# Loads of a batch of row pairs split by column halves in a tuned weight-gradient matmul

## The chip, the cores and the metric

One core of a Trainium2 chip. The metric is the device time of one execution, in microseconds (us). The kernel before takes 163.06 us, the median of two runs (162.97 and 163.16).

## The reference

```python
batch, m, k, n = 16, 512, 1024, 768      # input: [16, 512, 1024], grad_output: [16, 512, 768], float32

def reference(input, grad_output):
    return np.einsum('bmk,bmn->kn', input, grad_output).astype(np.float32)
```

With batch and m taken as one axis this is one matrix product: out[k, n] is the sum over 8192 rows of X[row, k] * G[row, n], with X of 8192 x 1024 and G of 8192 x 768. The kernel computes it in bf16 with float32 sums.

## The kernel before, in words

The 8192 rows are cut into 64 tiles of 128 rows, and these are taken two at a time: 32 pairs, numbered 0 to 31. A pair's rows lie in two tiles of on-chip memory (SBUF), `xp` (128 partitions x 2 x 1024, bf16) and `gp` (128 x 2 x 768, bf16). The DMA turns float32 into bf16 on the way.

*Loads.* POOL issues nearly all of them, in the order of the pairs (lines 108 to 126). From pair 2 on (`MERGED = 2`) a pair comes in two transfers: line 114 loads G, line 115 loads X. Partition p takes rows 2p and 2p+1 of the pair's 256, which lie side by side in memory, so that each partition reads one contiguous run (6 KB of G, 8 KB of X, float32). Pairs 0 and 1 come row tile by row tile (lines 119 and 121), and the first tile of G and the first two of X come as float32 on the queues of SP and ACT (lines 88 to 91) and are rounded by DVE and ACT (line 212). In the program as built, POOL's transfers take turns on eight semaphores: from the ninth on, each waits until the one eight before it has landed. A pair also waits for its buffer, of which there are 14 (`PAIRS_HELD`).

*Two kinds of pairs.* `LOADS` gives each pair a kind. An "s" pair (0 to 6, 30 and 31) is multiplied plainly, one row tile at a time. The output is cut into four quarters by halves of K and of N: A and B are the upper half of K, C and D the lower; A and C use the right half of G's columns (`LEFT` is `slice(NH, N)`), B and D the left. Each quarter is four matmuls of 128 x 384 per row tile (`Q = 4`), so 16 per tile and 32 per pair. A "P" pair (7 to 29) takes 7 products in place of 8, as Strassen's method does with 2 x 2 blocks, the blocks being the two row tiles and the two column halves: D, A and five more sums m, n, o, p and q, 28 matmuls in all. Its operands are sums and differences of the blocks. DVE makes them in five steps per pair, `sum_g1` (line 139) and `sum_g2` (144) from `gp`, `sum_x1` (149), `sum_x2` (153) and `sum_x3` (158) from `xp`. `sum_g1` reads all of `gp`, `sum_x1` all of `xp`; some products read the raw blocks (the function `operands`).

*Order.* `ORDER` is written out by hand: each step names a stream (A to D, m to q), the item up to which it goes on, and how its banks of PSUM are drained. A number ahead of the letter is how many sums (or later steps of putting the shares together) DVE does first. PE, DVE, ACT and POOL run the instructions in just this order (`manual_schedule`). PE accumulates a stream in four banks of PSUM (line 338). When a step closes, DVE adds the banks to float32 sums in SBUF (line 358) or ACT copies them there (354), having carried the earlier sum into the bank beforehand (297). Near the end DVE adds the shares of m to q to the quarters (195), and SP stores each finished block (line 361); the last block is multiplied and stored in two pieces (lines 393 to 403).

The lines that the steps below touch: 114 and 115 (the loads of pairs 2 to 31), 139 and 149 (the first sums on a pair's G and X), 338 (the matmuls and their weight loads).

Of the kernel before, what the change touches and what calls it, by code (L numbers as in the profile page):

```python
# [46 lines left out]
def kernel(  # L47
# [6 lines left out]
    nc = tc.nc  # L54
# [3 lines left out]
    B, M, K = input.shape  # L58
    _, _, N = grad_output.shape
    S = B * M // P  # L60
    KH = K // 2
    NH = N // 2
# [5 lines left out]
    X = input.rearrange("b m k -> (b m) k")  # L68
    G = grad_output.rearrange("b m n -> (b m) n")
# [38 lines left out]
    for u, kind in enumerate(LOADS):  # L108
        pool = pairs if u else head
        xp = pool.tile([P, 2, K], bf16, name="xp", tag="xp")  # L110
        gp = pool.tile([P, 2, N], bf16, name="gp", tag="gp")
        if u >= MERGED:
            rows = slice(2 * u * P, 2 * (u + 1) * P)
            nc.gpsimd.dma_start(out=gp, in_=G[rows, :].rearrange("(p m) n -> p m n", m=2))  # L114
            nc.gpsimd.dma_start(out=xp, in_=X[rows, :].rearrange("(p m) k -> p m k", m=2))  # L115
        for h in range(2):
            s = 2 * u + h
            if s > 0 and u < MERGED:
                nc.gpsimd.dma_start(out=gp[:, h, :], in_=G[s * P : (s + 1) * P, :])
            if s > 1 and u < MERGED:  # L120
                nc.gpsimd.dma_start(out=xp[:, h, :], in_=X[s * P : (s + 1) * P, :])
            if kind == "s":
                items.append(("s", xp[:, h, :], gp[:, h, :]))
        if kind == "P":
            items.append(("P", xp, gp))
        xg.append((xp, gp))
# [326 lines left out]
```

## Time and profile before

| what | value |
|---|---|
| median of 2 runs | 163.06 us (162.97 to 163.16) |
| the profiled execution: first to last instruction (span) | 161.1 us |
| granted TensorE clock | 1.000 |
| one load of G / of X from pair 2 on | 384 KB / 512 KB as written, median 16.7 / 16.8 us from issue to landing |
| POOL's issue of one such load | 0.53 us |
| one sum on DVE: line 139, 149 | 752 ns, 685 ns |
| matmul of 128 x 384, mean | 326 to 327 ns as shown; consecutive ones overlap |
| HBM read / written | 58.72 MB / 3.15 MB |

The profile is one execution, and the table's time of it is its span; the runs' time holds what lies around it too. PE is TensorE's matmuls, PEld its weight loads, DVE VectorE, ACT ScalarE, POOL GpSimd, SP SyncE. In the row of slices the span is cut into 40 equal parts, and a digit is the busy share in tenths (9 is 90% or more). The DMA queues' rows give packets, megabytes and the packets' time as a share of 16 engines; several packets can be under way on one engine, so that a share may exceed 100%. A waits row says who waited for whom: microseconds in total, times, longest. A timeline row is start, duration, engine, line, operation, and in brackets the idle time before it with what ended it.

### The profile page before, as it was taken

Reading aid. Unit: us, or ns where it says so; the run is one execution under the profiler, and the core shown is the slowest. Engines: PE = TensorE matmul, PEld = TensorE weight load, DVE = VectorE, ACT = ScalarE, POOL = GpSimd, SP = SyncE. Lnnn points to the kernel's source line nnn. Section 1 sums busy time; section 2 is a strip of 40 time slices with the busy share of each in tenths; the row PEclk is TensorE's granted clock in tenths of the full one; section 3 lists DMA queues with packets and bytes.
Section 4 is the critical chain, followed back from the end, with each engine's and each line's share of the span. In section 5 each row is a group of like instructions: output and inputs, shape, how many; then the busy total and the mean of one; then the engine's idle time right before and its main releaser. Section 6 shows DMA issues by size and latency. Waiting matters only on the chain.

```text
span 161.1 us, 2769 instructions
## 1 busy us (share of the span) xinstructions
PE 157.0 (97%) x944; PEld 92.7 (58%) x944; DVE 140.7 (87%) x267; ACT 117.9 (73%) x278; POOL 34.8 (22%) x69
## 2 busy tenths in 40 slices
PE   8999999999999999999999999999999999999991
PEld 3365665556555565556655665556655665555561
DVE  0645888889799999999998999999989998999982
ACT  3735357545589899978998897997795667988730
POOL 7442222122222212222212222221222100000000
PEclk9999999999999999999999999999999999999999
DMA  5999999999999999999999999999999999900695
GB/s 176 297 210 214 213 214 216 212 215 212 214 213 212 212 212 216 212 213 211 214 212 217 212 215 213 213 213 213 213 212 213 213 214 213 202 21 0 239 354 191
DMA packets 12398, 33.40 MB, mean 207 GB/s; under 512 B 1376, under 2 KB 4192, under 8 KB 12384
## 3 DMA queue, kind: packets, MB, share of 16 engines
q0 software_dynamic: 9360, 28.64, 89.8%
q1 hardware_dynamic: 2592, 3.47, 6.2%
q10 hardware_dynamic: 432, 1.11, 1.8%
q8 instruction: 7, 0.11, 0.3%
q14 instruction: 7, 0.06, 0.1%
HBM read 58.72 MB, written 3.15 MB: 384 GB/s over the span
## 4 chain that ended last, share of the span: by engine, by line
PE 97%; DVE 0%; issue 0%
PE bank L338 94%; PE bank L97 3%; PE bank L393 0%; DVE acc L401 0%
## 5 line engine op out<-in xcount | busy, mean ns | idle before, releaser
L338 PEld LDWEIGHTS <-xp 128*128 128x128 bf16 x650 | 63.3, 98 | 44.4 <-DVE xp L212 1.5
L338 PE MATMUL bank<-gp,xp 128*128 128x384 bf16 x468 | 81.0, 327 | 0.0
L354 ACT COPY macc<-bank 128x384 f32<-128x384 f32 x91 | 39.3, 491 | 9.8 <-PE bank L338 9.4
L358 DVE TENSOR_TENSOR acc<-bank,acc 128x384 f32<-128x384 f32 x80 | 39.6, 550 | 5.2 <-PE bank L338 4.8
L338 PEld LDWEIGHTS <-xe 128*128 128x128 bf16 x276 | 26.9, 98 | 17.9 <-DVE xe L149 0.2
L354 ACT COPY acc<-bank 128x384 f32<-128x384 f32 x57 | 24.7, 484 | 13.9 <-PE bank L338 13.9
L297 ACT COPY bank<-macc 128x384 f32<-128x384 f32 x73 | 33.0, 493 | 1.6 <-DVE acc L358 0.9
L338 PE MATMUL bank<-ge,xp 128*128 128x384 bf16 x182 | 33.5, 326 | 0.0
L338 PE MATMUL bank<-gp,xe 128*128 128x384 bf16 x184 | 32.4, 326 | 0.0
L297 ACT COPY bank<-acc 128x384 f32<-128x384 f32 x47 | 21.5, 491 | 8.7 <-DVE acc L358 7.0
L115 POOL DMA_DIRECT2D xp<-in_input_dram x30 | 16.0, 532 | 52.1 <-DMA xp<-in_input_dram 28.9
L114 POOL DMA_DIRECT2D gp<-in_grad_output_dram x30 | 16.0, 533 | 38.1 <-PE bank L338 17.2
L358 DVE TENSOR_TENSOR macc<-bank,macc 128x384 f32<-128x384 f32 x35 | 18.0, 550 | 0.8 <-PE bank L338 0.8
L139 DVE TENSOR_TENSOR ge<-gp 128x1152 bf16<-128x1152 bf16 x23 | 17.3, 752 | 0.6 <-DMA gp<-in_grad_output_dram 0.5
L149 DVE TENSOR_TENSOR xe<-xp 128x1024 bf16<-128x1024 bf16 x23 | 15.8, 685 | 2.1 <-DMA xp<-in_input_dram 2.1
L195 DVE TENSOR_TENSOR acc<-acc,macc 128x768 f32<-128x768 f32 (+1 forms) x20 | 16.1, 871 | 0.0
L338 PE MATMUL bank<-ge,xe 128*128 128x384 bf16 x92 | 15.9, 326 | 0.0
L158 DVE TENSOR_TENSOR xp<-xp 128x1024 bf16<-128x1024 bf16 x23 | 15.7, 684 | 0.0
L144 DVE TENSOR_TENSOR gp<-gp 128x768 bf16<-128x768 bf16 x23 | 12.7, 554 | 0.5
L153 DVE TENSOR_TENSOR xe<-xp 128x512 bf16<-128x512 bf16 x23 | 9.6, 418 | 0.0
L356 DVE COPY acc<-bank 128x384 f32<-128x384 f32 x6 | 3.2, 555 | 3.2 <-PE bank L338 3.1
L212 DVE CAST gp<-gf 128x192 bf16<-128x192 f32 (+1 forms) x2 | 0.7, 330 | 4.3 <-DMA gf<-in_grad_output_dram 4.3
(20 smaller groups left out, 19.9 us busy)
## 6 DMA issues: line engine op xcount, KB each, us to landing
xp<-in_input_dram POOLq DMA_DIRECT2D x30, 512.0 KB, 16.8
gp<-in_grad_output_dram POOLq DMA_DIRECT2D x30, 384.0 KB, 16.7
out_dram<-acc SPq DMA_DIRECT2D x15, 192.0 KB, 2.4
xf<-in_input_dram ACTq DMA_DIRECT2D x2, 512.0 KB, 4.8
gp<-in_grad_output_dram POOLq DMA_DIRECT2D x3, 192.0 KB, 6.4
xp<-in_input_dram POOLq DMA_DIRECT2D x2, 256.0 KB, 7.7
gf<-in_grad_output_dram SPq DMA_DIRECT2D x2, 192.0 KB, 4.2
out_dram<-acc SPq DMA_DIRECT2D x1, 128.0 KB, 1.9
```

Source lines behind the costliest of these rows:

```text
L114: nc.gpsimd.dma_start(out=gp, in_=G[rows, :].rearrange("(p m) n -> p m n", m=2))
L115: nc.gpsimd.dma_start(out=xp, in_=X[rows, :].rearrange("(p m) k -> p m k", m=2))
L139: nc.vector.tensor_add(out=ge.rearrange("p a n -> p (a n)"), in0=g[:, 0 : 3 * NH], in1=g[:, NH : 4 * NH])
L144: nc.vector.tensor_sub(out=g[:, 0::3, :], in0=g[:, 0::3, :], in1=g[:, 2:0:-1, :])
L149: nc.vector.tensor_add(out=xe[:, 0:2, :].rearrange("p a k -> p (a k)"), in0=xp[:, 0, :], in1=xp[:, 1, :])
L153: nc.vector.tensor_add(out=extra[i][0][:, 2, :], in0=xp[:, 0, 0:KH], in1=xp[:, 1, KH:K])
L158: nc.vector.tensor_sub(out=x[:, 1:3, :], in0=x[:, 1:3, :], in1=x[:, 0::3, :])
L195: op(out=dst, in0=dst, in1=src)
L297: nc.scalar.copy(out=bank, in_=sum_of(p, q))
L338: nc.tensor.matmul(bank, stat, mov, start=opening and j == 0 and not carried, stop=close and j == len(items_now) - 1, skip_group_check=car ...
L354: nc.scalar.copy(out=dst, in_=bank)
L358: nc.vector.tensor_add(out=dst, in0=bank, in1=dst)
```

## The change

From pair 2 on, G of a pair comes in two transfers, the column halves 0 to 383 and 384 to 767 of both of its rows in every partition, and X in two, columns 0 to 511 and 512 to 1023. The tiles, the sums, the matmuls and the order are the same. POOL issues the four in the order G first half, G second half, X first half, X second half. A partition's share of one transfer is now two runs (one per row) of 1536 bytes of G or 2048 bytes of X, as read. The eight semaphores stay eight.

```diff
         if u >= MERGED:
             rows = slice(2 * u * P, 2 * (u + 1) * P)
-            nc.gpsimd.dma_start(out=gp, in_=G[rows, :].rearrange("(p m) n -> p m n", m=2))
-            nc.gpsimd.dma_start(out=xp, in_=X[rows, :].rearrange("(p m) k -> p m k", m=2))
+            gsrc = G[rows, :].rearrange("(p m) n -> p m n", m=2)
+            xsrc = X[rows, :].rearrange("(p m) k -> p m k", m=2)
+            for c in (slice(0, NH), slice(NH, N)):
+                nc.gpsimd.dma_start(out=gp[:, :, c], in_=gsrc[:, :, c])
+            for c in (slice(0, KH), slice(KH, K)):
+                nc.gpsimd.dma_start(out=xp[:, :, c], in_=xsrc[:, :, c])
```

In after these two transfers of G stand in line 117 and those of X in line 119; later lines of before are four higher in after (338 is 342).

## The prediction

> **What bounds the kernel now.** I read the page from the top: engines, slices, the DMA queues, then the waits, then who waits for a transfer and when.
>
> ```profile
> PE 157.0 (97%) x944; PEld 92.7 (58%) x944; DVE 140.7 (87%) x267; ACT 117.9 (73%) x278; POOL 34.8 (22%) x69
> ...
> DMA  5999999999999999999999999999999999900695
> GB/s 176 297 210 214 213 214 216 212 215 212 214 213 212 212 212 216 212 213 211 214 212 217 212 215 213 213 213 213 213 212 213 213 214 213 202 21 0 239 354 191
> ...
> q0 software_dynamic: 9360, 28.64, 89.8%
> ```
>
> TensorE (PE) is busy for 157.0 of 161.1 us, and the chain that ended last is nearly all matmuls. Taken alone that says: only PE counts, transfers are free. The next row contradicts it. The DMA engines are full (9) from the second slice to the 35th, from the third to the 34th at a flat 210 to 217 GB/s: a slice is 161.1/40 = 4.03 us, so the loads run at their limit until about 141 us. That rate counts bytes written, as bf16; what is read, float32, is twice it.
>
> Is there slack between that stream and its users? The waits say no:
>
> ```profile
> DVE xe L149 <- DMA xp<-in_input_dram: 2.1, 4, 0.8
> ...
> PEld L338 <- DMA xp<-in_input_dram: 0.5, 2, 0.3
> ...
> DVE ge L139 <- DMA gp<-in_grad_output_dram: 0.5, 2, 0.2
> ```
>
> The waits are short but spread over the whole run. The timelines of DVE and of PE's weight loads, for 40 to 48 us and for 131 to 136 us:
>
> ```profile
> 42.86 0.69 DVE L149 TENSOR_TENSOR xe<-xp 128x1024 bf16<-128x1024 bf16 x1 [0.76 <-DMA xp<-in_input_dram]
> ...
> 133.60 0.69 DVE L149 TENSOR_TENSOR xe<-xp 128x1024 bf16<-128x1024 bf16 x1 [0.41 <-DMA xp<-in_input_dram]
> 133.62 1.58 PEld L338 LDWEIGHTS <-xp 128*128 128x128 bf16 x11 [0.23 <-DMA xp<-in_input_dram]
> ```
>
> The last sum pair that needs X is pair 29 (of 0 to 31). POOL issues its X at 116.89; with the median 16.8 us to landing that is 133.7, and at 133.60 and 133.62 both DVE and PE start on it, having waited. So the same stream that held DVE at 42.86 holds DVE and PE at 133.6: in 91 us no cushion has been built up. Two limits run level, PE's work and the load stream, and the order of PE is fixed by hand: a load that comes later moves everything behind it.
>
> POOL's issues tell how deep the queue is:
>
> ```profile
> 116.89 0.53 POOL L115 DMA_DIRECT2D xp<-in_input_dram  x1 [1.89 <-PE bank L338]
> 118.74 0.53 POOL L114 DMA_DIRECT2D gp<-in_grad_output_dram  x1 [1.32 <-DVE xe L153]
> ...
> xp<-in_input_dram POOLq DMA_DIRECT2D x30, 512.0 KB, 16.8
> ```
>
> The second line's releaser I do not use. A pair (512 + 384 = 896 KB) comes every 4.3 us (the X issues at 116.89 and 121.18); 16.8 us are four pairs, eight transfers in flight. In the built program the ninth and every later POOL transfer indeed waits for the semaphore of the one eight before it.
>
> **The change, part by part.** It starts at pair 2. Matmuls, sums and drains stay as they are and in the same order; bytes too.
>
> *Packets.* In before one partition's share of a pair's G is one run of 2 x 768 elements, of X one of 2 x 1024, so a transfer is 128 packets. The page's count agrees: 60 x 128 + 5 x 128 single-row ones + 65 x 16 completion writes = 9360. In after each transfer takes half of the columns of two rows: two runs in each partition, 256 packets, of 1536 bytes read (768 written) for G and 2048 (1024) for X. Per pair and DMA engine: 2 x 128/16 + 2 = 18 packets before, 4 x 256/16 + 4 = 68 after, 50 more. What does a packet cost beyond its bytes? Two stretches of full DMA engines with different packet sizes give it: 24 to 124 us (merged pairs), then 6.5 to 10.5 us (mostly single rows, 1536 and 2048 bytes written):
>
> ```profile
> DMA packets 6670, 21.30 MB, mean 213 GB/s; under 512 B 745, under 2 KB 745, under 8 KB 6661
> ```
>
> ```profile
> DMA packets 553, 0.84 MB, mean 209 GB/s; under 512 B 70, under 2 KB 366, under 8 KB 553
> ```
>
> Engine time is 1600 us in the first and 64 us in the second. With c ns per byte and o per packet: 21.30e6 c + 6670 o = 1.6e6; 209 GB/s for 4 us are 0.836e6 bytes, so 0.836e6 c + 553 o = 64,000. The first gives c = 0.0751 - 0.000313 o; put into the second, 62,800 + 291 o = 64,000 and o = 4.1 ns. The window 0.4 us later (518 packets, 208 GB/s) gives 5.8 in the same way. I take 4.5 ns, nearer the first, which holds more of the small packets. A pair then costs 50 x 4.5 = 0.22 us more, 4.53 in place of 4.3.
>
> Bounds. Below: 0, if the packets' overhead hides in a limit of the whole fabric. Above: the stores at the end are packets of 1536 bytes too (float32 both sides); from 150.5 to 157 us they move
>
> ```profile
> DMA packets 1657, 2.27 MB, mean 350 GB/s; under 512 B 182, under 2 KB 1656, under 8 KB 1656
> ```
>
> in 6.5 x 16 = 104 us of engine time. At c/2 = 0.037 ns per byte read, their bytes take 84 us and leave 20/1657 = 12 ns per packet. They write to HBM and have gaps between them, so I take this as an end only.
>
> The Trainium skill, "DMA: Bandwidth & Descriptors", section "Why small descriptors are slow", speaks against the change: a fixed three or so cycles per packet, and its fabric clock of 850 MHz makes that 3.5 ns, by which the sum would be 28 x 50 x 3.5 = 4.9 us. The windows above agree in size. "Perfetto Trace Analysis", section "DMA Optimizations", allows splitting so that some chunks start sooner where DMA engines are generally idle; here the slices show them full, so its condition isn't met.
>
> *On the path.* Pair 29's X is behind pairs 2 to 29, 28 pairs: 28 x 0.225 = 6.3 us later. PE and DVE have nothing in hand at that point (0.23 and 0.41 us of waiting), so all of it reaches the end. Late next are pairs 30 and 31 (X issued at 121.18 and 125.49, landing at about 138.0 and 142.3). Their first matmuls stand 86 and 67 before PE's end at 157.5 (counted in ORDER from A38 and A40), at 0.163 us each 143.5 and 146.6: 5.5 and 4.3 us of slack against 0.2 to 0.5 us more delay. They don't decide.
>
> *POOL.* 60 more issues. One takes 0.53 us with 128 runs; with 256 it lies between 0.53 and twice that, 1.06. Four per pair are 2.1 to 4.2 us, under the 4.53 us that the transfers take: covered, hardly so at the upper end. I take 0.8, and no cost.
>
> *Depth.* Eight in flight are now two pairs, about 9 us, not 16.8. The first POOL transfer, issued at 1.23 into an empty queue with the float32 loads beside it, lands 6.1 us later; POOL issues the one that waited for it at 7.62, a round of 6.4, under 9. The queue stays fed: no cost.
>
> *Waits.* Each first sum of G and of X (23 + 23) waits for two transfers, not one, which takes an added wait instruction on DVE; behind it stand DVE's drains of PSUM, and PE and ACT wait for those. POOL's wait instructions take 17 to 43 ns, so 0.8 to 2.0 us in all, in DVE time that the late stream leaves idle: 0 while it is late, up to 2.0 if it isn't. The first half of a pair's X lands about 1.1 us before the second. A single-row pair's first matmul uses only the first half of X, but the second sum, which holds DVE, takes both, and the rate stays: at most PE's 0.5 us of waits is saved.
>
> Sum: the profiled execution's span is 161.1, plus 6.3 is 167.4. The median 163.06 lies 1.9 above that span (the launch around it), so **169.4 us**.
>
> **Rivals.**
> 1. *Stream slower by more, at the stores' price.* For it: equal packet size. Against it: HBM writes, gaps. 28 x 50 x 12 ns = 17 us: 180.
> 2. *POOL becomes the bound.* If 256 runs cost more than 1.13 us per issue, four exceed 4.53 us. At 1.25 a pair takes 5.0: 28 x 0.7 = 20 us, 183. Against it: doubling all of 0.53 gives 1.06. For it: the trace has no transfer of two runs per partition.
> 3. *Not slower: packets are free.* If the flat 213 GB/s is a limit shared by all DMA engines, shorter packets hide in it; the stream keeps its 4.3 us, the early halves save up to 0.5 us, the added waits cost up to 2.0: 162.6 to 165, say 163. It is decided at 3.3/(28 x 50) = 2.3 ns per packet, 2% of the time. For it: the rate is flat within 2%. Against it: it fell to 208 and 209 when packets were shorter.
> 4. *Too shallow.* If issue to landing takes over 9 us even unqueued, the stream starves: at 10 us for eight transfers a pair takes 5.0, again 183. Against it: the 6.1 us above.
>
> **How the numbers follow.** Forecast 0.72 (packets at 3 to 9 ns: 28 x 50 x 3 and x 9 give 167 to 176), rival 1 0.08, rival 2 0.06, rival 3 0.11, rival 4 0.03. A difference of 2% is about what a measurement here tells from none. Slower by over 2%: 0.72 + 0.08 + 0.06 + 0.03 = 0.89, less 0.01 for a forecast that just misses it: 0.88. Within 2%: 0.10. Faster: 0.02, both from rival 3 and that 0.01. Range 165 to 178: it leaves out rival 3's lower part and the full price of rivals 1, 2 and 4.
>
> **What would show it.** Right: q0 with 120 x 256 + 640 + 125 x 16 = 33,360 packets at the same MB; full slices at about 203 GB/s until 147 us; time to landing near 9 us; waits of DVE and PE's weight loads for xp and gp, several us in all; PE busy still 157 us, so a smaller share. Wrong: the rate still 213 (rival 3); issues over 1.1 us and POOL nearly always busy (rival 2); DMA slices below 9 with POOL idle (rival 4). The step I trust least is o, from a 4 us window.

## The result, and the profile after

After the change the kernel takes 169.3 us (median of 2 runs, 169.17 to 169.43) against 163.06: the ratio is 1.038, with a 95% interval of 1.035 to 1.041. Slower by 3.8%. The profiled execution's span went from 161.1 to 167.4 us.

The rows of the page of after that answer to those of before (engines, slices, the load queue, the chain by engine):

```profile
PE 159.3 (95%) x944; PEld 91.7 (55%) x944; DVE 141.4 (84%) x267; ACT 118.4 (71%) x278; POOL 87.2 (52%) x129
...
DMA  5999999999999999999999999999999999940595
GB/s 183 289 203 192 202 204 204 203 202 203 204 203 202 203 204 203 204 203 203 204 204 202 204 203 202 204 203 203 203 203 206 201 203 204 202 68 0 191 355 206
...
q0 software_dynamic: 33360, 28.65, 106.9%
...
DMA 61%; PE 27%; issue 3%; DVE 3%; ACT 1%; POOL 1%; POOLq 0%; DVEq 0%
```

The same 28.65 MB come in 33,360 packets in place of 9360. The DMA engines' slices are full as before, up to the 35th, and move 203 GB/s in place of 213. A slice is now 4.19 us, so the stream ends at about 148 us in place of 141. The chain has changed its name: now 61% of it is transfers, and before it was nearly all PE:

```profile
PE 97%; DVE 0%; issue 0%
```

Who waits, from the waits of after:

```profile
DVE xe L153 <- DMA xp<-in_input_dram: 6.9, 12, 1.0
...
PEld L342 <- DMA xp<-in_input_dram: 2.2, 3, 1.1
...
DVE ge L143 <- DMA gp<-in_grad_output_dram: 2.1, 7, 0.4
```

DVE's first sum of X waited 2.1 us in 4 places before, 6.9 in 12 now; DVE's first sum of G 0.5 before, 2.1 now. And the last place where the stream decides, pair 29's X, from the timeline:

```profile
140.01 1.58 PEld L342 LDWEIGHTS <-xp 128*128 128x128 bf16 x11 [1.07 <-DMA xp<-in_input_dram]
...
140.06 0.69 DVE L153 TENSOR_TENSOR xe<-xp 128x1024 bf16<-128x1024 bf16 x1 [0.95 <-DMA xp<-in_input_dram]
```

These are the same two instructions that stood at 133.62 and 133.60. They start 6.4 and 6.5 us later, and the span is 6.3 us longer: what the stream loses until pair 29 is what the kernel loses.

### The profile page after: what moved, and what is told of

The parts are those of the page before. It is cut to its first block, busy times and chain, and to the rows that moved or that the text cites. A ratio compares the mean times of both kernels' runs of the same rounds, so it can differ in the third digit from the quotient of the medians.

```text
span 167.4 us, 2878 instructions
## 1 busy us (share of the span) xinstructions
PE 159.3 (95%) x944; PEld 91.7 (55%) x944; DVE 141.4 (84%) x267; ACT 118.4 (71%) x278; POOL 87.2 (52%) x129
## 3 DMA queue, kind: packets, MB, share of 16 engines
q0 software_dynamic: 33360, 28.65, 106.9%
## 4 chain that ended last, share of the span: by engine, by line
DMA 61%; PE 27%; issue 3%; DVE 3%; ACT 1%; POOL 1%; POOLq 0%; DVEq 0%
DMA xp<-in_input_dram 58%; PE bank L342 27%; DMA gp<-in_grad_output_dram 4%; DVE xe L153 1%; POOL xp L119 1%; ACT macc L358 1%; DVE macc L362 1%; PE bank L397 0%; DVE acc L405 0%; DVE xp L162 0%; ACT bank L301 0%; DVE gp L148 0%; DVE xe L157 0%; DVE ge L143 0%; DVEq L153 0%
## 5 line engine op out<-in xcount | busy, mean ns | idle before, releaser
L342 PEld LDWEIGHTS <-xp 128*128 128x128 bf16 x650 | 62.6, 98 | 49.2 <-DVE xp L162 3.2
L119 POOL DMA_DIRECT2D xp<-in_input_dram x60 | 42.1, 702 | 34.8 <-DMA xp<-in_input_dram 20.0
L117 POOL DMA_DIRECT2D gp<-in_grad_output_dram x60 | 42.1, 703 | 18.0 <-DMA gp<-in_grad_output_dram 6.4
L342 PE MATMUL bank<-ge,xp 128*128 128x384 bf16 x182 | 34.4, 326 | 1.3 <-DVE xp L162 0.9
L342 PE MATMUL bank<-gp,xe 128*128 128x384 bf16 x184 | 33.3, 326 | 1.3 <-DVE xe L153 1.3
```

The source lines that it names most:

```text
L117: nc.gpsimd.dma_start(out=gp[:, :, c], in_=gsrc[:, :, c])
L119: nc.gpsimd.dma_start(out=xp[:, :, c], in_=xsrc[:, :, c])
L342: nc.tensor.matmul(bank, stat, mov, start=opening and j == 0 and not carried, stop=close and j == len(items_now) - 1, skip_group_check=car ...
```

## The experiments

The theory: each packet costs some nanoseconds beyond its bytes, the load stream is the second bound that runs level with PE, and so the loss is the added price per pair times the 28 pairs up to pair 29. The rivals are named in the expectations: A, the number of transfers costs (issues, waits, half the bytes in flight); B, DVE's added waits; C, the reads' scattering in HBM; D, a cushion, so that only late pairs count. Each kernel is before with its two load lines exchanged. `gsrc` and `xsrc` are the views of G and X of the diff.

**e1, two transfers, packets as long as before.**

```diff
+for r in (slice(0, P // 2), slice(P // 2, P)):
+    nc.gpsimd.dma_start(out=gp[r], in_=gsrc[r])
+for r in (slice(0, P // 2), slice(P // 2, P)):
+    nc.gpsimd.dma_start(out=xp[r], in_=xsrc[r])
```

> Two transfers each for G and X from pair 2 on, as in the change, but split by partitions (0 to 63, 64 to 127): each partition's share stays one run of 6 or 8 KB, so the packets of a pair stay 16 per DMA engine and only the completion writes go from 2 to 4. Theory (each packet costs 4.6 ns beyond its bytes, 6.4 us over 28 pairs of 50 more packets): 28 x 2 x 4.6 = 0.3 us, 163.3, the rate still 212 to 213 GB/s. Rival A (the number of transfers costs: 60 more issues, completions, waits, half the bytes in flight): as the change, 169. Rival B (the added waits of DVE cost): up to 2 us, 165.

Measured: 164.33 us, ratio 1.0078 (1.0063 to 1.0093), 1.3 us. That is neither the theory's 0.3 nor rival A's 6. The load queue, 24 to 124 us, of before and then of e1:

```profile
q0 software_dynamic: 6661, 21.19, 106.7%
```

```profile
q0 software_dynamic: 7323, 20.98, 106.6%
```

A pair is 0.9175 MB, so it took 4.330 us in before and 4.373 here, 0.043 more; over 28 pairs that is 1.2 us, nearly all of the loss. So it is the stream again, not DVE's waits (which e1 has as the change does), and what is new in the stream is two completion writes per pair and engine: 21 ns each. Half the bytes in flight could have cost the same, but the packets' records in the two traces speak for the writes: in these 100 us a completion write (4 bytes) lasts 22 ns at the median in both, the data packets keep their 248 and 324 ns, and never are fewer than 16 packets under way on the 16 engines, so the queue didn't run short. The theory had priced such a write like any packet; that part of it falls.

**e2, one transfer, two runs per partition.** `"(p m) n -> p m n"` becomes `"(m p) n -> p m n"` in both loads.

> One transfer each for G and X as before, but partition p takes rows p and p+128 of the pair, so its share is two runs of 3 or 4 KB as read: 32 + 2 = 34 packets per pair and engine, 16 more than before. Theory: 28 x 16 x 4.6 ns = 2.1 us, 165.1, about 210 GB/s. Rival A: nothing, 163. The sum over rows is the same, in another grouping.

Measured: 164.79 us, ratio 1.0097 (1.0082 to 1.0113), 1.75 us. Rival A, which gave no change here, is out as the main cause. The same row and window:

```profile
q0 software_dynamic: 12418, 20.92, 113.4%
```

4.386 us per pair, 0.056 more for 16 packets: 3.5 ns each.

**e3, two transfers, split by rows.**

```diff
+for m in range(2):
+    nc.gpsimd.dma_start(out=gp[:, m, :], in_=gsrc[:, m, :])
+for m in range(2):
+    nc.gpsimd.dma_start(out=xp[:, m, :], in_=xsrc[:, m, :])
```

> Two transfers each, split by the two rows of a partition: one run of 3 or 4 KB as read per partition and transfer, 32 + 4 = 36 packets per pair and engine, 18 more. Theory: 28 x 18 x 4.6 ns = 2.3 us, 165.4, the same as e2 within 0.3. Rival A: as the change, 169.

Measured: 166.41 us, ratio 1.0202 (1.0183 to 1.0221), 3.4 us. It was expected to equal e2 and does not: the two further completion writes show, and a slower start, which the table below comes to.

```profile
q0 software_dynamic: 13018, 20.73, 113.3%
```

4.426 us per pair, 0.096 more. e1's 0.043 and e2's 0.056 make 0.099: the two prices add up.

**e4, one transfer, the change's packets.** The tiles get four column blocks of 384 (G) or 512 (X), 16 elements apart; sums and matmuls read the blocks in their places.

```diff
-PAIRS_HELD = 14
+PAIRS_HELD = 13
...
+            xp = Blocks(pool.tile([P, 4, KH + PAD], bf16, name="xp", tag="xp"), KH)
+            gp = Blocks(pool.tile([P, 4, NH + PAD], bf16, name="gp", tag="gp"), NH)
...
+            gsrc = G[rows, :].rearrange("(p m) (h n) -> p (m h) n", m=2, h=2)
+            xsrc = X[rows, :].rearrange("(p m) (h k) -> p (m h) k", m=2, h=2)
+            nc.gpsimd.dma_start(out=gp.all, in_=gsrc)
+            nc.gpsimd.dma_start(out=xp.all, in_=xsrc)
```

> One transfer each, read as one whole run per partition, but written as four blocks that lie 32 bytes apart (the tiles are padded, 13 pairs held in place of 14): 64 + 2 = 66 packets per pair and engine, 48 more, with the number of transfers, the depth in bytes and DVE's waits as before. Theory: 28 x 48 x 4.6 ns = 6.2 us, 169.2, about 203 GB/s. Rival A: 163. Rival C (the reads' scattering in HBM costs, not the packets): 163, since what is read together lies together.

Measured: 167.66 us, ratio 1.0278 (1.0262 to 1.0293), 4.6 us. The queue in 24 to 124 us of e4, then of after:

```profile
q0 software_dynamic: 23461, 20.38, 126.9%
```

```profile
q0 software_dynamic: 23953, 20.21, 126.7%
```

4.502 us per pair in e4, 0.172 more for 48 packets, 3.6 ns each; 4.540 in after, 0.210 more. The number of transfers, their bytes in flight and DVE's wait instructions are those of before, and what is read together lies together: rivals A, B and C all gave 163. e2 splits what is read and e4 what is written, at the same price. Packets by themselves make three quarters of the loss. The rest is the two completion writes: 0.172 + 0.043 = 0.215 against 0.210.

| kernel | packets, completion writes added per pair and engine | us per pair added (queue row) | x 28 | measured |
|---|---|---|---|---|
| e1 | 0, 2 | 0.043 | 1.2 | 1.3 |
| e2 | 16, 0 | 0.056 | 1.6 | 1.75 |
| e3 | 16, 2 | 0.096 | 2.7 | 3.4 |
| e4 | 48, 0 | 0.172 | 4.8 | 4.6 |
| after | 48, 2 | 0.210 | 5.9 | 6.2 |

e3 and after lie 0.7 and 0.3 us above the product. Much of that is lost at the start. From 13 to 17 us e3 moved 187 GB/s and after 190, where they later move 208 and 203: 0.4 and 0.3 us of stream. In before, e1, e2 and e4 these 4 us ran at 205 to 214 GB/s, within 1 GB/s of the later rate. Why halves that are also made of more packets are slow there, the runs do not tell.

**e5, e6 and e7, the change for some pairs.** The loads of the diff stand under `if u < 16:`, `if 16 <= u < 30:` or `if u >= 30:`, with the old two lines under `else:`.

> The change for pairs 2 to 15 alone, the rest as before. Theory (stream and PE run level, nothing is made up later): 14 x 50 x 4.6 ns = 3.2 us, 166.3, the same as e6. Rival D (there is a cushion that soaks up early lateness, only the end counts): under 1 us, 163 to 164.

> The change for pairs 16 to 29 alone. Theory: 14 x 50 x 4.6 ns = 3.2 us, 166.3. Rival D: the late half carries all of the loss, near 169.

> The change for pairs 30 and 31 alone. Theory (they have 4.3 to 5.5 us of slack, the split makes them 0.2 to 0.5 us later): no change, 163.1. A theory in which any late load counts: 0.5 us, 163.5.

Measured: e5 166.40 us, ratio 1.0211 (1.0196 to 1.0227); e6 165.86, 1.0180 (1.0163 to 1.0197); e7 163.03, 1.0007 (0.9996 to 1.0017). That is 3.4, 2.9 and 0.1 us on 162.97; e5 and e6 make up 6.3. By the table's 0.21 us per pair each would lose 2.9; e5, which has the split at the start, moved 180 GB/s from 13 to 17 us, and e6 211. Two stretches of e5, with the columns PE, PEld, DVE, ACT and POOL busy, clock, DMA share, GB/s:

```profile
24.00:75.00 51.00, 50.27 (x304) 29.10 (x303) 45.46 (x89) 37.65 (x89) 30.30 (x45) 1.00 1.27 203
75.00:135.00 60.00, 59.54 (x366) 35.28 (x364) 57.83 (x111) 51.34 (x121) 14.01 (x27) 1.00 1.07 213
```

Once the split pairs are through, the stream runs at 213 GB/s again, and still the 3.4 us are not made up in the 60 us that follow: a stream at its own limit has nothing to catch up with. Rival D is out. Pairs 30 and 31, which had 4.3 to 5.5 us of slack by the prediction's count, cost nothing that these runs can tell.

**e8 and e9, quarters: where the two covers end.** Each of G and X comes in four transfers, by columns in e8 (`t[:, :, c * w : (c + 1) * w]`, w a quarter of the columns), by partitions in e9 (`t[r : r + P // 4]`).

> Four transfers each for G and X from pair 2 on, by column quarters: 8 runs per partition of 768 or 1024 bytes as read, 128 + 8 packets per pair and engine. The runs so far give 3.4 to 3.9 ns for a data packet and about 25 ns for a completion write, so the stream alone would take 4.32 + 112 x 3.5 ns + 6 x 25 ns = 4.86 us per pair and the time 163 + 28 x 0.54 = 178. Issue-bound (POOL takes 0.70 us for 256 runs, as in the change): 8 x 0.70 = 5.6 us per pair, 163 + 28 x 1.28 = 199, POOL nearly always busy. Depth-bound (eight transfers in flight are one pair; a round of 6.4 us as for the first transfer): 6.4 per pair, 221, POOL and DMA both idle in part.

> Four transfers each by partitions (32 at a time), whole runs: 16 + 8 packets per pair and engine, so the stream alone would take 4.32 + 6 x 25 ns = 4.47 us per pair: 163 + 28 x 0.15 = 167.2. POOL's issues at 0.51 us (as with 64 runs) are 4.1 us per pair, under the stream. Depth-bound (eight in flight are one pair, 4.47 us of stream): if the round from issue to the next issue is 6.4 us, 6.4 per pair and 221; any round over 4.5 us shows as DMA slices under full with POOL idle.

e8 took 203.2 us (ratio 1.246, 1.242 to 1.250). Its page, the engines and the slices of POOL, and its POOL timeline from 80 us:

```profile
PE 169.0 (84%) x944; PEld 92.3 (46%) x944; DVE 143.1 (71%) x267; ACT 119.5 (59%) x278; POOL 170.1 (84%) x249
...
POOL 7589999997999999969999999999999989990000
```

```profile
79.85 2.79 POOL L118 DMA_DIRECT2D xp<-in_input_dram  x4
82.64 2.78 POOL L118 DMA_DIRECT2D gp<-in_grad_output_dram  x4
85.42 1.39 POOL L118 DMA_DIRECT2D xp<-in_input_dram  x2
88.34 1.40 POOL L118 DMA_DIRECT2D xp<-in_input_dram  x2 [1.53 <-issue]
```

Four issues take 2.8 us, eight 5.6, with no gap between them: POOL sets the pace, as the 199 of the issue-bound case had it; pauses such as the 1.53 us come on top. From 24 to 124 us POOL is busy for 94.8 us. The DMA engines' slices read 9 there all the same, at 157 GB/s: a full slice is no proof that the DMA engines are the limit.

e9 took 180.8 and 184.2 us, where the stream alone gave 167 and a round of 6.4 us gave 221. Neither number is right. The profile is of the longer run. Its slices of the DMA engines, 60 to 120 us, and the issue after the dip:

```profile
DMA  9999999999999999995899999999999999999999
```

```profile
83.14 1.45 POOL L118 DMA_DIRECT2D gp<-in_grad_output_dram  x3 [0.27 <-PE bank L341]
87.67 0.49 POOL L118 DMA_DIRECT2D gp<-in_grad_output_dram  x1 [3.08 <-issue]
```

POOL stands still for 3.08 us after 84.59, and the DMA engines dip at its end (the 19th slice begins at 87). With one pair in flight such a pause reaches the stream. But dips are rare, while the rate over these 60 us is 177 GB/s; most of e9's loss is in slices that are shown full. The packets' records tell a little more: from 60 to 120 us the median data packet lasts 248 and 324 ns as in before, but 6% of them last over half as long again, up to 1.7 us, and an engine that holds such a packet counts as busy. What holds these packets, and what ends POOL's pauses, is open.

## Why the prediction was right, step by step

*The bound.* Right: two limits ran level, and the stream's delay at pair 29 came through whole (6.4 us there, 6.3 in the span). e5 and e6 show that it adds up pair by pair, e7 that it ends at pair 29.

*The price of a packet.* The sum was right, its parts were not. It had 50 packets at 4.5 ns, 0.225 us per pair; measured are 48 at 3.5 ns and two completion writes at 21 ns, 0.21 us. The two windows could not separate the two kinds, since completion writes were 11% of the packets in one (745 of 6670) and 13% in the other (70 of 553): each fitted price was a mixture, and as the change adds fewer writes than that (2 in 50), part of the fit's nearness was luck. So was a part of the total: the pairs' price gives 5.9 of the 6.2 us, and the slower start, which the sum had at nothing, makes up for what is missing to its 6.3. The Trainium skill, "DMA: Bandwidth & Descriptors", section "Why small descriptors are slow", has about three cycles per packet. At the fabric clock of 850 MHz in the same page's "Specifications" that is 3.5 ns, an estimate; e2 and e4 agree with 3.5 and 3.6.

*Rival 1, the stores' price of 12 ns.* Out: the packets of these loads cost 3.5 ns. What else was in the 12, the gaps or the writes to HBM, no run separates.

*POOL.* The cover held. An issue takes 0.70 us with 256 runs, between the bounds and below the 0.8 that I took; four are 2.8 of 4.54 us. Rival 2's point, 1.13 us, is the right kind of point: e8 passes it by number, with eight issues of 0.70 us (5.6 us) against about 4.9 that its stream would take, and is bound there.

*Depth.* The cover held once the stream was running: 8.8 us from issue to landing, and no loss of rate beyond the packets' and writes' price. From 13 to 17 us the rate was lower, as said; whether the depth did that, no run shows. e9 shows that one more halving is too much, though not by the arithmetic of one round. The sign that was set for rival 4, slices below 9, would have missed most of it.

*Added waits.* Nothing that can be told from zero: e1 has all of them, and the stream explains 1.2 of its 1.3 us (1.0 to 1.5 by the interval). On DVE one wait instruction takes 21 ns in after. The early halves bought nothing that shows.

*Rival 3, packets are free.* Out: the rate fell to 203 GB/s, as the prediction had it, and the stream ended at 148 us (147 forecast). PE's busy time was to stay at 157 us; it reads 159.3 with the same 944 matmuls, for a reason that no run tested.

## What to carry to other kernels

Ask of a stream that runs full whether its users have any cushion: compare when a late load lands with when it is first used, not only the share that the busiest engine has. Where they run level, a split that brings data earlier in pieces makes all of it later by the price of its packets and completions, and the loss adds up over the stretch until the last load that somebody waits for. Here the split had nothing to gain, and with the runs per partition kept whole (e1) it lost a fifth as much. Don't take a full slice alone as proof of a full stream: see whether its rate is the best that these packets reach.

## What was not expected of the hardware

A completion write costs a DMA engine about 21 ns in a full queue, six packets' worth (e1). An issue on POOL takes 0.49 us with 32 runs (e9), 0.53 with 128 and 0.70 with 256. In e8, where PE is busy for 84% of the span, the mean granted clock of the profiled run is 0.966, against 1.000 in before; in e9's, with PE busy for 89%, it is 1.000. What lowers it, no run shows.
